# The sixth depthwise tile of a Conformer convolution: from TensorE to VectorE, ScalarE and POOL together

## The chip, the cores and the metric

One core of a Trainium2 chip runs the whole program in one launch. The metric is device time in microseconds (us) from start to end of one execution. A kernel is run several times, and medians are compared.

## The reference, cut to what matters

The program is a two-layer decoder trunk on 512 tokens of width 1024, in f32: each layer has two SwiGLU feed-forward blocks around a mixer, and a gated input embedding behind them. The mixer of layer 0 is a Conformer convolution, and the change lies inside it:

```python
def conformer_conv(h, w_pw1, b_pw1, w_dw, b_dw, ln_g, ln_b, w_pw2, b_pw2):
    u = h @ w_pw1 + b_pw1                     # 1024 -> 2048 channels
    a, g = jnp.split(u, 2, axis=-1)
    u = a * jax.nn.sigmoid(g)                 # the gate
    u = lax.conv_general_dilated(             # one causal filter of 31 taps per channel
        u, w_dw[:, None, :], window_strides=(1,), padding=[(CONV_KERNEL - 1, 0)],
        dimension_numbers=('NWC', 'WIO', 'NWC'), feature_group_count=D_MODEL) + b_dw
    mu = jnp.mean(u, axis=-1, keepdims=True)  # LayerNorm over the 1024 channels
    var = jnp.mean(jnp.square(u - mu), axis=-1, keepdims=True)
    u = (u - mu) * lax.rsqrt(var + LN_EPS) * ln_g + ln_b
    return jax.nn.silu(u) @ w_pw2 + b_pw2
```

The norm needs all 1024 channels of a token, so the second projection can't begin before the last channel's filter is done.

## The kernel before

Channels lie on the 128 partitions and tokens on the free axis: eight channel tiles c = 0 to 7 of 128 x 512. Every matrix product is made of three matmuls of rounded halves (`mm3`, lines 355 to 357). Weights come in units of 128 x 1024 in the order of use (`raw`, L243 on the queue of SP), and each is split in two: the high half by ScalarE (`wh`, L291), the low half by VectorE or, for the second projection of this stage, by POOL (`wl`, L293). Five split buffers go round, so a split waits until TensorE is done with the unit five before.

`conv` runs over the tiles. For each it makes the first projection (two banks of PSUM, 48 matmuls), then the gate (`glu`): VectorE scales (L732, L714), ScalarE applies the sigmoid (L715), VectorE multiplies. From there the tile's filter goes one of three ways, by the table `CONV_ON`:

- `pe`: the gated tile (L719) is written to DRAM (`ud`, L720) and read back rearranged by phase of the token (`uu`, L721). TensorE then makes the 31 taps with 36 matmuls against expanded taps (`tw`, four tiles of 576 KB per channel tile, L705; filter L817). ScalarE empties the bank (L822), and the result goes through DRAM again (`yd` L823, `y` L824).
- `dve`: the gated tile is written to SBUF with 30 zeros ahead (`u`, three buffers, L725, zeros L724). VectorE adds tap by tap in two PSUM banks (L744, L746), and joins them (L749, L750).
- `pool`: ScalarE scales the shifted tile by a tap (L759), POOL adds it to `y` (L760).

Behind each filter stands `tally`: the tile is added to a running sum (`total`, L774). After the first four tiles `centre` takes an estimate of the mean from the sum with a matmul (L785); from then on each tile also gets that mean taken off (L797), is squared on ScalarE (L803), and the square is added up (L804, the first four times on POOL).

The generators of `dve` and `pool` are pumped a few steps at a time between the projections (`PUMP`), the rest in a loop at the end of `conv`. While the last filters run, TensorE makes 16 small tiles of the input embedding (`z_tiles`; `fill`): each is 6 matmuls on `zp` into a bank of its own, emptied by ScalarE (L649) and sent to DRAM (L650). The end of the stage is: the sum's matmul (L903), the sums per token (L444, once for the total and once for the squares, six matmuls of `fill` between), the root on POOL (L437), and then per tile two steps of VectorE, the SiLU, the split (L925 to L929) and the second projection, whose matmuls are those on `tw` at L355 to L357.

What is written in this order is put through a list scheduler when the program is built. It fixes one order per engine and per queue, and on the chip each engine and queue works through its own order; an instruction that waits holds all behind it on its engine. `high_priority(FIN_PRI)` and `issue_after` are hints to that scheduler.

Of the kernel before, what the change touches and what calls it, by code (L numbers as in the profile page):

```python
# [14 lines left out]
AF = mybir.ActivationFunctionType  # L15
OP = mybir.AluOpType
# [5 lines left out]
TAPS = 31  # L22
X_W1, WARM = 4, 18
OUTS = 2
CONV_FIN = 0
PE_LATE = (3, 4, 5)
FIN_PRI = 100
CALM = ("ple_w_gate", "conv_w_pw2")
FIN_AT = (1, 3)
LATE, OUT_POOL, OUT_AFTER = 3, (1, 4), 2  # L30
PH, LAGS = 4, 9
CONV_ON = ("pool", "dve", "dve", "pe", "pe", "pe", "pe", "pe")
TAPS_AT = {max(0, c - 2): (c,) for c in range(8) if CONV_ON[c] == 'pe'}
TWB, PUMP = 8, {"dve": 5, "pool": 3, "pe": 0}
CENTRED = 2
FILL = (6, 0, 4, 3)
EARLY, SQP, PUMP2, ZIN = 4, 4, (12, 0), 6
CG, SP = 128 // PH, S // PH
# [18 lines left out]
def plan():  # L57
# [79 lines left out]
    for i in range(L):  # L137
        ffn(1, i)
        if i == 0:
            conv(0)  # L140
        else:
            nsa()
        ffn(2, i)
        full("ple_w_gate", i, KD, range(KD))
# [40 lines left out]
def phases(t):  # L185

    return t.rearrange("p (s r) -> p r s", r=PH)


def drain(gen):  # L190
    for _ in gen:
        pass


class Kern:
# [505 lines left out]
    def taps(self, c):  # L701

        T = [self.ptile("tw", TWB, 128 * LAGS) for _ in range(PH)]
        for q in range(PH):
            self.nc.sync.dma_start(T[q], self.a["tw"][CONV_ON[:c].count("pe"), q])  # L705
        return T

    def glu(self, c, pa, pg, ta=None):
# [4 lines left out]
        with self.tc.high_priority(FIN_PRI):  # L713
            nc.vector.tensor_tensor(pg, pg, self.R, op=OP.mult)  # L714
            nc.scalar.activation(pg, pg, AF.Sigmoid, bias=self.col("conv_b_pw1", KD + c))  # L715
            if CONV_ON[c] == "pe":
                u = self.ptile("uu", 2, PH * (SP + LAGS - 1)).rearrange("p (q s) -> p q s", q=PH)
# [35 lines left out]
    def dw_pool(self, c, u, y):  # L753
# [7 lines left out]
            yield  # L761
        self.tally(c, y)

    def tally(self, c, y):

        nc, b = self.nc, self.col("conv_b_dw", c)
        if not self.done:
            self.total = self.ptile("sum", 4)
            nc.vector.tensor_scalar(self.total, y, b, None, op0=OP.add)
        else:  # L770
            old = self.total
            if len(self.done) == EARLY:
                self.total = self.ptile("sum", 4)
            nc.vector.scalar_tensor_tensor(self.total, y, b, old, op0=OP.add, op1=OP.add)  # L774
        self.done.append((c, y))
        if self.mid is not None:
            self.square(c, y)
# [49 lines left out]
    def conv(self, nxt):  # L827

        nc = self.nc
# [3 lines left out]
        self.ud, self.yd = (self.dpool.tile([D, S], F32, name=n) for n in ("ud", "yd"))  # L833
        fin = self.rfin(self.acc)
        self.T, self.late, self.done, self.mid, self.squares, self.sqp = {}, [], [], None, None, SQP
        work = {"dve": self.dw_dve, "pool": self.dw_pool, "pe": self.dw_pe}
        queues = {on: [] for on in work}

        def pump(which, n):
            q = queues[which]  # L840
            while n > 0 and q:
                if next(q[0], q) is q:
                    q.pop(0)
                else:
                    n -= 1

        def filt(c, pa, pg, ta=None):
            u = self.glu(c, pa, pg, ta)
            Y.append(self.ptile("y", KD))
            queues[CONV_ON[c]].append(work[CONV_ON[c]](c, u, Y[c]))  # L850

        for c in range(KD):
# [13 lines left out]
            for p, o in ((pa, c), (pg, c + KD)):  # L866
# [5 lines left out]
                if p is pa:  # L872
                    ta = self.scaled(pa)
                if p is pg and c - 2 in PE_LATE:
                    drain(queues["pe"].pop(0))
                for on in queues:
                    pump(on, PUMP[on])
            filt(c, pa, pg, ta)
            if CONV_ON[c - 1] == "pe" and c - 1 not in PE_LATE:
                drain(queues["pe"].pop(0))  # L880

        def late(n):
            for _ in range(n):
                self.tally(*self.late.pop(0))
# [4 lines left out]
        fill = itertools.chain(*[self.z_tiles(i, ZP[i]) for i in range(L)])  # L889
        for _ in range(FILL[3]):  # L890
            next(fill)
# [1 line left out]
            drain(queues["pe"].pop(0))  # L893
        pump("dve", PUMP2[1])
        while any(queues.values()):
            for on, n in (("dve", 7), ("pool", 3)):
                pump(on, n)
        late(len(self.late))
        for _ in range(FILL[0]):
            next(fill)  # L900
        off, pt = self.bank(), self.bank()
        with self.tc.high_priority(FIN_PRI):
# [3 lines left out]
            u = self.tiny.tile([128, 4], F32, name="u", tag="u")  # L906
# [7 lines left out]
        nc.vector.tensor_tensor(off, off, self.mid, op=OP.subtract)  # L914
        for _ in range(FILL[1] + FILL[2]):
            next(fill)
# [4 lines left out]
        for c in range(KD):  # L921
            pair = self.ptile("tw", TWB, 128 * LAGS, F32R)
            h, l = pair[:, :512], pair[:, 512:1024]
            with self.tc.issue_after(ui if c < CENTRED else vi):
                nc.vector.tensor_tensor(Y[c], Y[c], off, op=OP.subtract)  # L925
# [546 lines left out]
def pack(inputs):  # L1472
# [17 lines left out]
    dw = taps[lag + PH].reshape(PH, LAGS, PH, KD, PH, CG).transpose(3, 4, 5, 0, 1, 2)  # L1490
    tw = np.zeros((CONV_ON.count("pe"), PH, CG, PH, LAGS, CG, PH), np.float32)
    for n, c in enumerate(c for c in range(KD) if CONV_ON[c] == "pe"):
# [33 lines left out]
```

## Time and profile before

| what | value |
|---|---|
| median of 3 runs | 2022.3 us (2020.97 to 2022.66) |
| the profiled execution's own time | 2022.25 us |
| its span in the trace | 2020.4 us |
| mean granted TensorE clock | 0.995 |
| busy: TensorE / VectorE / ScalarE / POOL | 99% / 77% / 54% / 16% |
| the convolution's stage | about 360 to 562 us of the span |

All times of trace rows count from the span's start. In rows of a timeline the columns are start, length, engine, line, operation, output<-inputs, shapes and count; merged rows give the length of the whole run of instructions. A bracket at the end tells how long the engine had been idle and what released it. PE is TensorE, DVE VectorE, ACT ScalarE, SPq the queue of DMAs that SP issues. In rows of the chain of work each row is a piece of the path that ended last. In rows of busy time by stretch the columns are the stretch, then its length, then busy time and number of instructions of PE, PEld, DVE, ACT and POOL, the granted clock, the DMA engines' share and GB/s.

### The profile page before, as it was taken

To read this page: it belongs to the slowest core of one execution; us is meant where nothing else is said; L and a number is where in the kernel's file an instruction comes from. 1 tells how busy PE (TensorE), PEld (TensorE's weight loads), DVE (VectorE), ACT (ScalarE), POOL (GpSimd) and SP (SyncE) were. 2 spreads that over 40 slices of the span, in tenths; PEclk is the share of its full clock that TensorE was granted. 3 is DMA by queue.
4 is the path that set the end of the run, shared out by engine and by line. 5 is a ranking of instruction groups with operands and counts; after the bars stand their busy time and mean duration, and the time that the engine had idled before them with its cause. 6 is when DMAs were issued, how large, how long until landed. Compare 5 with 4: busy or idle time off the path is not lost.

```text
span 2020.4 us, 32792 instructions
## 1 busy us (share of the span) xinstructions
PE 1993.4 (99%) x12534; PEld 1789.1 (89%) x12534; DVE 1559.0 (77%) x2751; ACT 1100.5 (54%) x1972; POOL 330.7 (16%) x365
## 2 busy tenths in 40 slices
PE   8999999999999999999999999999999999999998
PEld 7989899888789898988999989887888789898987
DVE  8869777795687796877968868647989796886875
ACT  7535445663565363545644535437888674463543
POOL 0000000352300000012000000557666200000022
PEclk9999999999999999999999999999999999999999
DMA  4332323466425244243232322463323023232241
GB/s 167 107 99 100 126 75 103 180 203 210 136 98 172 89 142 127 97 136 115 84 120 90 117 92 95 152 191 105 93 87 100 29 95 124 95 115 94 94 141 58
DMA packets 79484, 235.16 MB, mean 116 GB/s; under 512 B 8848, under 2 KB 16160, under 8 KB 79328
## 3 DMA queue, kind: packets, MB, share of 16 engines
q1 hardware_dynamic: 78368, 230.69, 34.8%
q8 instruction: 98, 1.61, 0.3%
q0 software_dynamic: 816, 2.33, 0.3%
q14 instruction: 58, 0.48, 0.1%
q10 hardware_dynamic: 144, 0.07, 0.0%
HBM read 214.66 MB, written 16.29 MB: 114 GB/s over the span
## 4 chain that ended last, share of the span: by engine, by line
PE 88%; DVE 7%; ACT 2%; DMA 1%; issue 1%; SPq 0%; DVEq 0%; POOL 0%; ACTq 0%
PE b L355 27%; PE b L356 27%; PE b L357 27%; PE b L817 2%; PE b L1176 1%; PE b L1238 1%; DMA raw<-in_w 1%; PE b L1257 1%; PE b L1115 1%; PE b L1258 1%; DVE t L1241 1%; DVE s L414 1%; DVE wl L293 1%; DVE t L481 0%; DVE acc L431 0%
## 5 line engine op out<-in xcount | busy, mean ns | idle before, releaser
L355 PE MATMUL b<-s,wh 128*128 128x256 f32 (+1 forms) x1408 | 447.9, 319 | 5.0 <-ACT wh L291 4.3
L356 PE MATMUL b<-s,wh 128*128 128x256 f32 (+1 forms) x1408 | 447.0, 318 | 1.3 <-DVE s L414 0.9
L357 PE MATMUL b<-s,wl 128*128 128x256 f32 (+1 forms) x1408 | 445.3, 318 | 0.5 <-DVE wl L293 0.4
L291 ACT ACTIVATE wh<-raw 128x1024 fp32r<-128x1024 f32 (+1 forms) x251 | 263.6, 1053 | 259.1 <-PE b L356 173.6
L355 PE MATMUL b<-px,wh 128*128 128x256 f32 (+1 forms) x1112 | 321.8, 290 | 0.8 <-ACT G L502 0.8
L356 PE MATMUL b<-px,wh 128*128 128x256 f32 (+1 forms) x1112 | 321.3, 289 | 0.8 <-DVE px L490 0.8
L357 PE MATMUL b<-px,wl 128*128 128x256 f32 (+1 forms) x1112 | 321.2, 289 | 0.0
L293 DVE TENSOR_TENSOR wl<-raw,wh 128x1024 fp32r<-128x1024 f32 (+1 forms) x205 | 251.3, 1227 | 69.6 <-ACT wh L291 68.9
L355 PEld LDWEIGHTS b<-s,wh 128*128 128x128 f32 x1408 | 267.7, 190 | 24.0 <-ACT wh L291 5.2
L356 PEld LDWEIGHTS b<-s,wh 128*128 128x128 f32 x1408 | 267.7, 190 | 19.9 <-DVE s L414 2.5
L357 PEld LDWEIGHTS b<-s,wl 128*128 128x128 f32 x1408 | 266.9, 190 | 18.3 <-DVE wl L293 1.1
L357 PE MATMUL b<-hid,wl 128*128 128x512 f32 x704 | 275.0, 393 | 0.0
L356 PE MATMUL b<-hid,wh 128*128 128x512 f32 x704 | 274.8, 392 | 0.0
L355 PE MATMUL b<-hid,wh 128*128 128x512 f32 x704 | 269.3, 390 | 0.0
L293 POOL TENSOR_TENSOR wl<-raw,wh 128x1024 fp32r<-128x1024 f32 (+1 forms) x53 | 128.4, 2427 | 709.4 <-ACT wh L291 709.2
L502 ACT ACTIVATE G<-b 128x256 f32<-128x256 f32 x400 | 144.6, 377 | 134.7 <-PE b L357 118.2
L355 PEld LDWEIGHTS b<-px,wh 128*128 128x128 f32 x1112 | 209.7, 189 | 6.4 <-ACT G L502 1.4
L356 PEld LDWEIGHTS b<-px,wh 128*128 128x128 f32 x1112 | 209.5, 188 | 5.9 <-DVE px L490 1.0
L357 PEld LDWEIGHTS b<-px,wl 128*128 128x128 f32 x1112 | 209.2, 188 | 3.8
L356 PEld LDWEIGHTS b<-hid,wh 128*128 128x128 f32 x704 | 132.2, 188 | 29.2
L355 PEld LDWEIGHTS b<-hid,wh 128*128 128x128 f32 x704 | 132.2, 188 | 28.5
L357 PEld LDWEIGHTS b<-hid,wl 128*128 128x128 f32 x704 | 132.1, 188 | 27.4
(246 smaller groups left out, 3644.7 us busy)
## 6 DMA issues: line engine op xcount, KB each, us to landing
raw<-in_w SPq DMA_DIRECT2D x255, 512.0 KB, 3.3
rawx<-in_w SPq DMA_DIRECT2D x80, 512.0 KB, 3.2
tw<-in_tw SPq DMA_DIRECT2D x20, 576.0 KB, 6.8
skew<-table SPq DMA_DIRECT2D x16, 320.0 KB, 5.9
z<-t SPq DMA_DIRECT2D x16, 256.0 KB, 2.3
hid<-z SPq DMA_DIRECT2D x16, 256.0 KB, 4.2
tt<-skew SPq DMA_DIRECT2D x16, 256.0 KB, 2.8
wr<-in_w SPq DMA_DIRECT2D x8, 512.0 KB, 4.2
```

The costliest lines, as they stand in the source:

```text
L291: nc.scalar.activation(h[:, c], t[:, c], AF.Copy)
L293: eng.tensor_tensor(l[:, c], t[:, c], h[:, c].bitcast(F32), op=OP.subtract)
L355: mm(out, sh, mh, start=start, stop=False, **how)
L356: mm(out, sh, ml, start=False, stop=False, **how)
L357: self.lastmm = mm(out, sl, mh, start=False, stop=stop, **how).ins
L414: b = nc.vector.scalar_tensor_tensor(view(l), x, g, view(h.bitcast(F32)), op0=OP.mult, op1=OP.subtract)
L502: copy = lambda o, x: nc.scalar.activation(o, x, AF.Copy)
L817: nc.tensor.matmul(p[:, q * SP:q * SP + SP], T[q][:, d * 128:d * 128 + 128], u[:, q, o:o + SP], start=d == 0, stop=d == LAGS - 1)
L1115: nc.tensor.matmul(P[mh][:, :124], w, B[kk // 4][:, kk % 4, :], start=kk == 0, stop=kk == 15)
L1176: nc.tensor.matmul(p[:, :32 - lo + nk], Q, KT[:, i, "sw".index(b), lo:32 + nk], start=i == 0, stop=i == 1)
L1238: nc.tensor.transpose(p[:, a * 128:a * 128 + 128], J[a, b][:, kt * 128:kt * 128 + 128], self.ident)
L1241: nc.vector.tensor_tensor(l, p, h.bitcast(F32), op=OP.subtract)
```

## The change

Tile 5 (the sixth) leaves the way `pe` for a fourth way, `mix`. Its gated tile is written to SBUF like a `dve` tile's. VectorE makes taps 0 to 15 in two PSUM banks; ScalarE scales for taps 16 to 30, and POOL adds 14 of these to `y` (the first is written there); then ScalarE brings the second bank to SBUF, POOL adds it, and VectorE adds the first bank to `y`.

```diff
-PE_LATE = (3, 4, 5)
+PE_LATE = (3, 4)
-CONV_ON = ("pool", "dve", "dve", "pe", "pe", "pe", "pe", "pe")
+CONV_ON = ("pool", "dve", "dve", "pe", "pe", "mix", "pe", "pe")
-TWB, PUMP = 8, {"dve": 5, "pool": 3, "pe": 0}
+TWB, PUMP = 8, {"dve": 5, "pool": 3, "pe": 0, "mix": 2}
+MIXED = 16
...
+    def dw_mix(self, c, u, y):
+        nc = self.nc
+        acc, n = [self.bank(), self.bank()], MIXED
+        for j in range(n):
+            a, w = acc[j % 2], self.dwc[:, c, j:j + 1]
+            if j < 2:
+                nc.vector.tensor_scalar(a, u[:, j:j + 512], w, None, op0=OP.mult)
+            else:
+                nc.vector.scalar_tensor_tensor(a, u[:, j:j + 512], w, a, op0=OP.mult, op1=OP.add)
+            if n + j < TAPS:
+                t = self.tmp() if j else y
+                nc.scalar.activation(self.rs(t), phases(u[:, n + j:n + j + 512]), AF.Copy,
+                                     scale=self.dwc[:, c, n + j:n + j + 1])
+                if j:
+                    nc.gpsimd.tensor_tensor(y, y, t, op=OP.add)
+            yield
+        t = self.tmp()
+        nc.scalar.activation(self.rs(t), phases(acc[1]), AF.Copy)
+        nc.gpsimd.tensor_tensor(y, y, t, op=OP.add)
+        nc.vector.tensor_tensor(self.rs(y), phases(acc[0]), self.rs(y), op=OP.add)
+        self.tally(c, y)
...
-        work = {"dve": self.dw_dve, "pool": self.dw_pool, "pe": self.dw_pe}
+        work = {"dve": self.dw_dve, "pool": self.dw_pool, "pe": self.dw_pe, "mix": self.dw_mix}
...
-            for on, n in (("dve", 7), ("pool", 3)):
+            for on, n in (("dve", 7), ("pool", 3), ("mix", 4)):
```

In the changed kernel lines 37 to 763 stand one lower than in the kernel before, and those behind 787 24 lower: L760 is now L761, L822 is L846, L903 is L927. The new way has L772 and L774 (taps on VectorE), L777 (scaling), L780 (POOL's add), L783 to L785 (the join).

The scheduler's order is moved at three places. The first is VectorE around the gate of tile 6 (its product is `t478_4431` before and `t474_4421` now). Before, taps of tile 2 (`u404`) stand around it:

```order
L774 SCALAR_TENSOR_TENSOR sum449_4265<-y422_4110,small_74,sum449_4265 128x512
L746 SCALAR_TENSOR_TENSOR b450_4267<-u404_3999,dwc_3711,b450_4267 128x512
L746 SCALAR_TENSOR_TENSOR b451_4268<-u404_3999,dwc_3711,b451_4268 128x512
L719 SCALAR_TENSOR_TENSOR t478_4431<-t478_4431,small_74,b476_4400 128x512
L746 SCALAR_TENSOR_TENSOR b450_4267<-u404_3999,dwc_3711,b450_4267 128x512
```

Now, with taps of tile 5 (`u457`) among them:

```order
L774 SCALAR_TENSOR_TENSOR b476_4432<-u457_4361,dwc_3711,b476_4432 128x512
L798 SCALAR_TENSOR_TENSOR sum445_4257<-y418_4102,small_74,sum445_4257 128x512
L774 SCALAR_TENSOR_TENSOR b477_4433<-u457_4361,dwc_3711,b477_4433 128x512
L747 SCALAR_TENSOR_TENSOR b446_4259<-u404_3999,dwc_3711,b446_4259 128x512
L720 SCALAR_TENSOR_TENSOR t474_4421<-t474_4421,small_74,b472_4390 128x512
```

From the join of tile 1 (L750) up to this gate VectorE has 10 taps of tile 5 that it had not, and 5 fewer of tile 2, which come later.

The second place is ScalarE behind the emptying of tile 7's filter bank. Before, the squares of tiles 5, 6 and 7 and the emptying of the `fill` banks follow:

```order
L822 ACTIVATE t514_4802<-b513_4765 128x512
L803 ACTIVATE t515_4808<-y462_4374 128x512
L803 ACTIVATE t516_4813<-y484_4525 128x512
L291 ACTIVATE wh520_4832<-raw87_4569 128x1024
L803 ACTIVATE t517_4818<-y493_4648 128x512
L649 ACTIVATE t519_4828<-b518_4821 128x512
```

Now the last seven scalings of tile 5 and its second bank stand there, the squares and the banks behind them:

```order
L846 ACTIVATE t517_4783<-b516_4746 128x512
L777 ACTIVATE t518_4788<-u457_4361,dwc_3711 128x512
L777 ACTIVATE t519_4792<-u457_4361,dwc_3711 128x512
L777 ACTIVATE t520_4796<-u457_4361,dwc_3711 128x512
L777 ACTIVATE t521_4800<-u457_4361,dwc_3711 128x512
L777 ACTIVATE t522_4804<-u457_4361,dwc_3711 128x512
L777 ACTIVATE t523_4808<-u457_4361,dwc_3711 128x512
L292 ACTIVATE wh531_4846<-raw87_4583 128x1024
L777 ACTIVATE t524_4812<-u457_4361,dwc_3711 128x512
L783 ACTIVATE t525_4816<-b477_4433 128x512
L292 ACTIVATE wh540_4892<-raw88_4715 128x1024
L827 ACTIVATE t526_4822<-y458_4364 128x512
```

So seven of the fifteen scalings can't begin before TensorE has ended the filter of tile 7. The third place is POOL at the same time. Before:

```order
L804 TENSOR_TENSOR sum499_4704<-sum499_4704,t505_4726 128x512
L293 TENSOR_TENSOR wl520_4833<-raw87_4569,wh520_4832 128x1024
L293 TENSOR_TENSOR wl529_4879<-raw88_4734,wh529_4878 128x1024
L437 TENSOR_TENSOR r_4909<-v_4905,power_78 128x4
L293 TENSOR_TENSOR wl540_4946<-raw89_4836,wh540_4945 128x1024
```

Now:

```order
L780 TENSOR_TENSOR y458_4364<-y458_4364,t521_4800 128x512
L294 TENSOR_TENSOR wl531_4847<-raw87_4583,wh531_4846 128x1024
L780 TENSOR_TENSOR y458_4364<-y458_4364,t522_4804 128x512
L294 TENSOR_TENSOR wl540_4893<-raw88_4715,wh540_4892 128x1024
L780 TENSOR_TENSOR y458_4364<-y458_4364,t523_4808 128x512
L780 TENSOR_TENSOR y458_4364<-y458_4364,t524_4812 128x512
L784 TENSOR_TENSOR y458_4364<-y458_4364,t525_4816 128x512
L438 TENSOR_TENSOR r_4923<-v_4919,power_78 128x4
```

Eight adds of tile 5 are left at that point (the first three, on `t518` to `t520`, stand just ahead of these rows), and two weight splits stand among them. On TensorE only the four rows of tile 5's filter are gone from between the first projection of tile 7 and the filter of tile 6; the 36 matmuls of `fill` between the filter of tile 7 and L903 stay where they were. On SP's queue the four `tw` loads and the four trips through DRAM of tile 5 are gone.

## The prediction

> **What bounds the kernel now.** I read the page's head first, then the table of busy time over the convolution, then what TensorE waits for there, then the chain of work.
>
> ```profile
> span 2020.4 us, 32792 instructions
> PE 1993.4 (99%) x12534; PEld 1789.1 (89%) x12534; DVE 1559.0 (77%) x2751; ACT 1100.5 (54%) x1972; POOL 330.7 (16%) x365
> sum 220.00, PE 219.01 PEld 185.47 DVE 158.10 ACT 127.62 POOL 75.43; mean PE 9.95 PEld 8.43 DVE 7.19 ACT 5.80 POOL 3.43
> 450.00:460.00 10.00, 10.00 (x64) 8.98 (x63) 10.00 (x15) 3.62 (x6) 0.51 (x2) 1.00 0.72 236
> PE b L355 <- ACT tw L928: 1.0, 1, 1.0
> ```
>
> The third row is 360 to 580 us: TensorE idles 1.0 us in 220, one wait at the start of the second projection. So the stage is bound by TensorE's work, and work taken from it is worth its length, provided nothing else becomes late. VectorE is the first candidate: in 450 to 460 (fourth row) it is busy throughout.
>
> ```profile
> 464.96 16.08 PE b L817 x144
> 481.04 0.86 PE b L785 x2
> 481.90 0.79 PE b L444 x8
> 487.01 8.04 PE b L817 x72
> 503.49 0.86 PE b L903 x2
> 504.34 0.79 PE b L444 x8
> 506.63 0.79 PE b L444 x8
> 517.36 1.20 PE b L355 x4
> ```
>
> These are pieces of the chain. The first row is tiles 5 and 6 back to back, the fourth tile 7. From the end of tile 7's filter (487.01 + 8.04 = 495.05) to L903 lie 8.44 us, filled by 36 matmuls of `fill`. That is all the cover that the last tally has.
>
> **The change, term by term.** *Removed.* Half of the first row, **-8.04 us** on the path. The four 576 KB loads and the trips through DRAM of tile 5 go from SP's queue; none was on the chain, so by themselves they bring nothing. L822 of tile 5 goes too.
>
> *Tile 6 moves up.* Its filter now stands at 464.96, where tile 5's stood. Is its input there? It comes from the gate on VectorE and two transfers.
>
> ```profile
> 437.90 1.06 DVE L750 TENSOR_TENSOR y<-b,t 128x512 f32<-128x512 f32 x1
> 442.17 4.69 DVE L746 SCALAR_TENSOR_TENSOR b<-u,dwc,b 128x512 f32<-128x512 f32 x7
> 459.01 0.73 DVE L719 SCALAR_TENSOR_TENSOR t<-t,small,b 128x512 f32<-128x512 f32 x1
> 472.41 0.75 DVE L719 SCALAR_TENSOR_TENSOR t<-t,small,b 128x512 f32<-128x512 f32 x1 [0.73 <-ACT b L715]
> 457.13 0.33 SPq L243 DMA_DIRECT2D raw<-in_w  x1
> 457.56 0.86 SPq L705 DMA_DIRECT2D tw<-in_tw  x2
> 459.77 0.33 SPq L720 DMA_DIRECT2D ud<-t  x1
> 465.34 0.37 SPq L721 DMA_DIRECT2D uu<-ud  x1
> 473.19 0.33 SPq L720 DMA_DIRECT2D ud<-t  x1
> 475.53 0.57 SPq L721 DMA_DIRECT2D uu<-ud  x1
> DMA to landing us min/median/max: 2.6/3.0/7.3
> ```
>
> The last row is that of `uu`. Between L750 and this gate the order has 10 taps more and 5 fewer; a tap takes 4.69 / 7 = 0.67, so 3.35, and the gate of tile 5 writes `u` instead of `t`, 0.4 more (1.12 against 0.74, below). There is no slack on VectorE to take that in, so tile 6's gate ends near 459.74 + 3.7 = 463.4. Before, from issuing `ud` to issuing `uu` took 5.57 for tile 6, behind three weight and tap loads, and 2.34 for tile 7, with free engines. Now two loads are ahead instead of three, and `ud` comes 3.7 later, so they are mostly through by then: I take 2.4, nearest tile 7's row. Landing at 463.4 + 2.4 + 3.0 = 468.8 gives a wait of 3.8; a little of the gate's delay is doubtful, and I take **+3.5** (ends: 0 if the transfers were as early as the filter, 7.1 with 5.57). Nothing else can run in it: TensorE's order has only this filter, then L785, then `fill`. Tile 7's gate is later by about as much (476), its transfers end at 476 + 2.4 + 3.0 = 481.4, and its filter starts at 464.96 + 3.5 + 8.04 + 0.86 + 0.79 + 4.3 of `fill` (481.90 + 0.79 to 487.01) = 482.5: just in time, no cost.
>
> *The clock.* A wait has a second price.
>
> ```profile
> 45.76 0.39 PE L355 MATMUL b<-s,wh 128*128 128x256 f32 x1 [3.10 <-ACT wh L291]
> 47.00:48.00 1.00, 1.00 (x5) 1.00 (x6) 1.00 (x3) 1.00 (x4) 0.00 (x0) 0.50 0.63 254
> 49.00:50.00 1.00, 1.00 (x8) 1.00 (x8) 1.00 (x3) 0.07 (x1) 0.00 (x0) 0.74 0.80 238
> 1582.40 0.69 PE L1238 MATMUL b<-ident,e 128*128 128x128 f32 x2 [2.41 <-POOL e L1218]
> 1588.00:1589.00 1.00, 1.00 (x4) 0.76 (x3) 0.97 (x3) 0.30 (x1) 1.00 (x4) 0.53 0.00 0
> ```
>
> After 3.10 us idle the granted clock (third figure from the end) was 0.50 and was back to 1.00 in the course of 49 to 50, 3.9 us after the restart by the 0.74; after 2.41 us idle it stayed low to 1589, 6.6 us. Half speed for 3.9 us loses 1.95. I charge **+1.9** for tile 6's wait (ends 0 and 3.3).
>
> The Trainium skill, TensorE: Matmul & The Clock Gate, section "What's actually happening", says that the array gets half of the pulses after an idle window of some 3.4 us and all again after about as long a busy one, in windows that run freely. By that rule a wait of 3.5 may or may not fill a window, and the sum would be without the 1.9 where it doesn't; the 2.41 row shows a drop after less, so the measurement speaks for charging it.
>
> *The tail of tile 5.* Everything that tile 5 adds to VectorE beside the two gates lies behind them and before L785, in time that was idle (the 9.41 us that VectorE waited for the centre, first row below). But seven scalings are queued on ScalarE behind the emptying of tile 7's bank, and eight adds and two splits on POOL behind these.
>
> ```profile
> 482.57 1.42 DVE L797 SCALAR_TENSOR_TENSOR y<-y,small,sum 128x512 f32<-128x512 f32 x2 [9.41 <-ACT sum L787]
> 414.34 6.80 ACT L759 ACTIVATE t<-u,dwc 128x512 f32<-128x512 f32 x6
> 495.15 0.60 ACT L822 ACTIVATE t<-b 128x512 f32<-128x512 f32 x1 [2.85 <-PE b L817]
> 504.88 1.08 ACT L291 ACTIVATE wh<-raw 128x1024 fp32r<-128x1024 f32 x1
> L760 POOL TENSOR_TENSOR y<-y,t x30: 1292/1300/2201, 383.7 to 448.8; 128x512 f32<-128x512 f32 x30
> L760 POOL TENSOR_TENSOR y<-y,t 128x512 f32<-128x512 f32 x30 | 44.6, 1488 | 33.2 <-ACT t L759 31.3
> L293 POOL TENSOR_TENSOR wl<-raw,wh 128x1024 fp32r<-128x1024 f32 x6 | 14.4, 2392 | 34.2 <-ACT wh L291 34.2
> L750 DVE TENSOR_TENSOR y<-b,t x2: 1064/1084/1103, 437.9 to 486.6; 128x512 f32<-128x512 f32 x2
> L725 DVE SCALAR_TENSOR_TENSOR u<-t,small,b 128x512 f32<-128x512 f32 x3 | 3.4, 1123 | 0.1
> L804 DVE TENSOR_TENSOR sum<-sum,t 128x512 f32<-128x512 f32 x3 | 2.1, 692 | 3.2 <-ACT t L803 3.1
> L774 DVE SCALAR_TENSOR_TENSOR sum<-y,small,sum x7: 737/752/1767, 452.1 to 500.8; 128x512 f32<-128x512 f32 x7
> ```
>
> Let E be the end of tile 7's filter. ScalarE empties its bank by E + 0.6, the first scaling ends at E + 1.8, six are through at E + 7.4 (6.80 / 6 = 1.13 each), the high half of a split at E + 8.4, the seventh scaling at E + 9.6, the bank copy at E + 10.7, the second high half at E + 11.8. POOL's four adds end at E + 1.8 + 4 x 1.30 = E + 7.0; it then waits until E + 8.4 for ScalarE, splits 2.4 to E + 10.8, adds to E + 12.1, splits 2.4 to E + 14.5, adds three times to E + 18.4. VectorE joins (1.08) to E + 19.5. Then come, one after another, the tally of tile 5 and its square's input (0.75 each), the same for tile 6, an add of squares (0.7) and the tally of tile 7: 4 x 0.75 + 0.7 + 0.75 = 4.5, and L903 starts at E + 24.0. It started at E + 8.44, so **+15.6** (lower end: the adds without the splits between, 8 x 1.30 from E + 1.8, 4.8 - 1.4 - 0.1 less, about +11; upper end: adds at the mean of 1.49, +1.5 more, +17). POOL's mean is the value under VectorE's load; in the tail VectorE waits for POOL, so I take the median.
>
> By the Trainium skill, GPSIMD Engine Reference, section "1. Specifications", POOL shares its SBUF interfaces with VectorE, with contention where that has two SBUF inputs; nothing of VectorE runs beside the tail's adds, so the sum by that rule is the same one with 1.30.
>
> *Behind L903.* TensorE has been idle for some 15 us, so the half clock is all but sure here. L903, L444, six matmuls and L444 of the squares took 506.63 - 503.49 = 3.14; with 3.9 us at half speed this becomes about 4.95: **+1.8** (ends 0.9, the emptying of a bank that now waits behind tile 7's square on ScalarE, and 3.0). From there to 517.36 VectorE and ScalarE set the pace (the 1.0 us wait), so slower `fill` matmuls are hidden.
>
> Sum: -8.04 + 3.5 + 1.9 + 15.6 + 1.8 = **+14.8 us**, on 2022.25 of the profiled execution (span 2020.4); the median of the runs, 2022.3, is the same within 0.05. Forecast **2037 us**, slower by 0.7%. A measurement of this kernel can tell about 0.2%, 4 us, from no change.
>
> **Rivals.**
>
> *The transfers are hidden and the clock forgives.* Tile 6's input arrives in time, nothing drops there: -8.04 + 15.6 + 0.9 = +8.5, 2031. For it speaks that fewer loads share the queue; against it that the gate alone is 3.7 late where the chain had 465.34 + 3.0 = 468.3 even before, which lies behind 464.96. Chance 0.12.
>
> *The removal pays.* The tail is hidden and 8.04 us are won: 2014. It decides at a tail of 8.44 + 8.04 = 16.5 us from E: below this the kernel is faster, and each microsecond of wait ahead takes one off. Even with both splits behind all adds, the eight adds, the lead of 1.8 and VectorE's 5.6 make 17.8. It needs scalings that run ahead of tile 7's filter, and ScalarE's order forbids that. Chance 0.04.
>
> *Break-even.* Tail near 18 and no wait of tile 6: -8.04 + 9.6 = +1.5, 2024. It needs the splits to cost nothing. Chance 0.05.
>
> *The shared port.* VectorE and POOL slow each other: POOL's adds took up to 2.2, and a tally 1.77 against 0.75. If this also hits the gate of tile 6 (four to five instructions at 1.0 more) and the adds run at 1.6: +14.8 + 2.4 + 4 = +21, 2043. For it: adds of tile 5 now run beside VectorE from 450 on. Against: most of VectorE's work then is taps, which took 0.67 each beside POOL at 442. Chance 0.09.
>
> **How the numbers follow.** The forecast holds 0.70, with its own range 2031 to 2041 from the ends above (no clock drop at tile 6 and a short wait; or a wait of 7). The first rival lies at 2031 and the port at 2043, and the range 2029 to 2042 leaves out the removal that pays, break-even and half of the port: under 0.2. Slower by over 0.2%: 0.70 + 0.12 + 0.09 and a little of break-even, 0.92; same 0.04; faster 0.04.
>
> **What would show it.** In the changed kernel's trace: L841 in three stretches of 8 us and the one of tile 6 starting near 468, with a wait for `uu` ahead; the granted clock at 0.50 behind it; L927 starting 24 us behind the end of the last L841, with a wait of some 15 us for VectorE, and VectorE's L785 waiting as long for POOL; the two L294 on POOL between the adds. The prediction is wrong if L927 follows its `fill` matmuls without a wait, or if TensorE's order at run time lets other work into the gap.

## Result, and the profile after

The changed kernel takes 2041.7 us (median of 4 runs, 2038.8 to 2043.5) against 2021.6 beside it: ratio 1.0095, 95% interval 1.0083 to 1.0107. That is 20 us slower, where 14.8 was forecast; the time lies 0.3 us inside the upper end of the range, 2029 to 2042. The profile below is of the slowest of the four executions (2043.5 us).

The page's head of the changed kernel:

```profile
span 2041.7 us, 32691 instructions
PE 1992.1 (98%) x12462; PEld 1786.4 (87%) x12462; DVE 1570.8 (77%) x2768; ACT 1117.5 (55%) x1987; POOL 350.3 (17%) x380
```

What its TensorE waited for between 360 and 600 us (total, times, longest):

```profile
PE b L927 <- DVE sum L798: 14.9, 1, 14.9
PE b L841 <- DMA uu<-ud: 7.1, 1, 7.1
```

Pieces of its chain of waits (start, length, what):

```profile
462.96 0.66 DVE t L720
463.63 5.67 DMA ud<-t
469.32 2.69 DMA uu<-ud
472.15 9.99 PE b L841 x72
488.09 8.05 PE b L841 x72
519.45 2.05 PE b L927 x2
521.50 1.50 PE b L445 x8
525.76 1.50 PE b L445 x8
```

TensorE is busy 1.3 us less in all and the span is 21.3 us longer: the time is waiting and slow clock, not work. Two waits are new. Tile 6's filter starts at 472.15 and not in tile 5's old place at 464.96; it then takes 9.99 in place of 8.04. L927 starts 23.3 us behind the end of tile 7's filter (488.09 + 8.05 = 496.14), where 8.44 had been.

The tail of tile 5, from the timelines of ScalarE, POOL and VectorE:

```profile
496.23 0.60 ACT L846 ACTIVATE t<-b 128x512 f32<-128x512 f32 x1 [2.78 <-PE b L841]
496.72 6.78 ACT L777 ACTIVATE t<-u,dwc 128x512 f32<-128x512 f32 x6
504.52 2.36 POOL L294 TENSOR_TENSOR wl<-raw,wh 128x1024 fp32r<-128x1024 f32 x1 [1.11 <-ACT wh L292]
506.85 1.25 POOL L780 TENSOR_TENSOR y<-y,t 128x512 f32<-128x512 f32 x1
508.06 2.33 POOL L294 TENSOR_TENSOR wl<-raw,wh 128x1024 fp32r<-128x1024 f32 x1
513.03 1.26 POOL L784 TENSOR_TENSOR y<-y,t 128x512 f32<-128x512 f32 x1
514.33 0.69 DVE L785 TENSOR_TENSOR y<-b,y 128x512 f32<-128x512 f32 x1 [23.05 <-POOL y L784]
```

It is the order that was foreseen: emptying, six scalings, the splits between the adds, and VectorE waiting 23.05 us for POOL.

The stage in stretches of four us (busy time of TensorE, its weight loads, VectorE, ScalarE and POOL, then granted clock, share of the DMA engines, GB/s), behind the restart at 519.45:

```profile
520.00:524.00 4.00, 4.00 (x13) 2.85 (x12) 1.86 (x3) 3.34 (x7) 0.00 (x0) 0.50 0.35 130
524.00:528.00 4.00, 4.00 (x15) 3.52 (x14) 0.70 (x3) 1.29 (x4) 0.00 (x0) 0.50 0.89 329
528.00:532.00 4.00, 4.00 (x14) 3.09 (x14) 4.00 (x9) 2.36 (x4) 1.02 (x1) 0.71 0.12 46
```

TensorE is busy in every microsecond from 520 on and still gets half the clock until about 530.3 (0.71 x 4 = 2.84, so 2.3 of the last four us at half), 10.9 us after it restarted.

The ledger of the stage, from the end of the projections to the start of the second one (517.36 before, 537.53 after, +20.2): filter removed -8.0, wait for `uu` +7.1, slow filter of tile 6 +1.95, tail +14.9, from L927 to the second projection +4.2. Sum 20.1. The remaining microsecond of the span lies scattered behind the stage.

### The profile page after: what moved, and what is told of

The parts are those of the page before. It is cut to its first block, busy times and chain, and to the rows that moved or that the text cites. A ratio compares the mean times of both kernels' runs of the same rounds, so it can differ in the third digit from the quotient of the medians.

```text
span 2041.7 us, 32691 instructions
## 1 busy us (share of the span) xinstructions
PE 1992.1 (98%) x12462; PEld 1786.4 (87%) x12462; DVE 1570.8 (77%) x2768; ACT 1117.5 (55%) x1987; POOL 350.3 (17%) x380
## 4 chain that ended last, share of the span: by engine, by line
PE 64%; DVE 11%; ACT 2%; issue 2%; DMA 1%; POOL 1%; SPq 0%; DVEq 0%; ACTq 0%; POOLq 0%
PE b L356 20%; PE b L357 20%; PE b L358 20%; DVE t L1265 1%; DVE b L747 1%; PE b L841 1%; DVE wl L294 1%; DVE e L1218 1%; PE b L1200 1%; PE b L1139 1%; ACT e L1220 0%; DVE s L415 0%; PE b L1262 0%; ACT t L1264 0%; DVE ect L1259 0%
```

## Experiments

The first three columns of the table come from all runs of a kernel; each ratio is to the kernel before in the same call, whose median was 2022.0 to 2022.5 for the experiments. The other columns come from one profile each, and a single execution can lie some us from its median (experiment 6's profile took 2045.5). "uu" is the wait of tile 6's filter and the filter's length by the timeline (8.20 with the whole clock, where the chain has 8.04, so that the changed kernel's 1.95 counts as 1.8 here); "tail" is the time from the end of tile 7's filter to L927 (8.27 before, by the rows of the timeline); "after" is the time from L927 to the second projection's first matmul.

```
kernel                          median   ratio (95%)               uu             tail    after
before                          2021.6   1                         0 + 8.2         8.3    14.0
changed                         2041.7   1.0095 (1.0083, 1.0107)   7.1 + 10.0     23.3    18.1
1 steps earlier                 2041.5   1.0095 (1.0080, 1.0110)   3.6 + 9.9      22.2    19.7
2 steps later, gate first       2046.6   1.0120 (1.0105, 1.0135)   2.1 + 9.9      32.4    19.7
3 splits on VectorE             2038.2   1.0078 (1.0063, 1.0093)   7.0 + 9.9      19.7    19.3
4 TensorE kept busy             2037.2   1.0076 (1.0059, 1.0093)   3.8 + 9.9      23.7    14.6
5 all steps ahead               2029.6   1.0037 (1.0024, 1.0049)   5.6 + 11.2     11.2    17.0
6 uu first                      2041.3   1.0090 (1.0074, 1.0105)   6.9 + 10.7     23.3    18.4
7 removal alone                 2021.1   0.9995 (0.9986, 1.0004)   3.6 + 11.0      8.3    14.0
8 all ahead, fill and uu first  2026.2   1.0022 (1.0013, 1.0031)   2.7 + 9.7      11.2    17.0
9 taps loaded later             2042.9   1.0102 (1.0088, 1.0115)   5.0 + 11.0     23.3    18.6
10 joining ahead too            2023.1   1.0006 (0.9997, 1.0015)   6.4 + 10.0      8.3    14.0
11 10 with fill and uu first    2019.7   0.9988 (0.9979, 0.9996)   2.5 + 9.7       8.3    14.0
12 10 with fill, two taps later 2021.3   0.9994 (0.9985, 1.0003)   3.9 + 10.9      8.3    14.0
```

The theory at the outset: the tail comes from where tile 5's last steps stand in the queues, and the other loss from tile 6's input. Rivals: the steps are too much work wherever they stand, or VectorE and POOL slow each other.

### 1. The steps written earlier

```diff
         self.centre()
+        pump("mix", MIXED + 1)
         pump("dve", PUMP2[0])
```

> The tail of tile 5 comes from where its last steps are written (seven scalings stand on ScalarE behind the emptying of tile 7's bank), not from how long the scalings and adds take. With all of them written ahead of it, L927 should start about 8.4 us behind the end of tile 7's filter, as in the kernel before (8.44), with no wait of its own (14.9 now); the clock behind it then stays whole, since TensorE is no longer idle ahead of it. Left over are the removed filter (-8.04), the wait of tile 6's filter (+7.1) and its slow clock (+1.95), so about 2021.6 + 1.0 = 2023 us (2021 to 2026). Rival: the scalings, the adds or the crowding of VectorE by POOL are simply too long for the stage; then more than half of the 14.9 us stays in front of L927 and the time is above 2031.

The order was as meant: all scalings stood ahead of the emptying of tile 7's bank. It brought nothing. From the timelines of ScalarE and TensorE:

```profile
475.29 0.66 ACT L716 ACTIVATE b<-b,small 128x512 f32<-128x512 f32 x1 [8.54 <-DVE b L715]
483.25 8.00 ACT L777 ACTIVATE t<-u,dwc 128x512 f32<-128x512 f32 x7
507.37 0.61 ACT L846 ACTIVATE t<-b 128x512 f32<-128x512 f32 x1
499.89 0.79 PE L356 MATMUL b<-zp,wh 128*128 128x512 f32 x1 [6.20 <-DVE y L785]
514.49 2.04 PE L928 MATMUL b<-sum,meanr 128*128 128x512 f32 x2 [4.46 <-DVE sum L798]
```

The seven scalings still stood behind tile 7's gate, for which ScalarE idled 8.54 us, and behind the squares, so they began at 483.25 and not 496.7. What they gained, two others lost: tile 5's two PSUM banks were held until its joining, so `fill` found no bank (6.20), and tile 7's own emptying stood on ScalarE behind the squares of tiles 5 and 2 and three emptyings of `fill` banks until 507.37. The tail is 22.2, by another road. My expectation was wrong, and by this run alone the rival "too much work" would stand.

### 2. The same, with none of tile 5's taps ahead of tile 6's gate

```diff
-TWB, PUMP = 8, {"dve": 5, "pool": 3, "pe": 0, "mix": 2}
+TWB, PUMP = 8, {"dve": 5, "pool": 3, "pe": 0, "mix": 0}
```

on top of the edit above.

> As with all steps of tile 5 written ahead of tile 7's emptying, and besides none of its VectorE taps ahead of tile 6's gate (ten stand there in the changed kernel). The gate on VectorE should end some 3.3 us sooner, tile 6's filter wait about 3.8 us rather than 7.1, so the time is 2 to 4 us under that of the version with the steps early alone: about 2019 us (2017 to 2023). Rival: the wait hangs on the two transfers' own length, not on the gate; then both versions agree within 1 us. A second way to lose: 16 taps on VectorE behind the gate end late, tile 5's join holds L927 back, and the time is above 2025.

What TensorE waited for between 430 and 600 us:

```profile
PE b L356 <- DVE y L785: 7.8, 1, 7.8
PE b L356 <- ACT t L783: 7.3, 1, 7.3
PE b L841 <- DMA uu<-ud: 2.1, 1, 2.1
```

The gate came 3.9 us sooner (`ud` issued at 459.74, 463.63 in the changed kernel) and the wait for `uu` fell to 2.1. TensorE waited for both of tile 5's banks, 7.3 us for the one that L783 frees and 7.8 for the other, where experiment 1 had one wait of 6.2, and the tail grew to 32.4. The second way to lose that was named is what happened.

### 3. Two of POOL's splits made on VectorE

```diff
+ON_DVE = [j for j, u in enumerate(UNITS) if u[0][0][0] == "conv_w_pw2"][1:3]
...
+        calm = calm and j not in ON_DVE
         eng = nc.gpsimd if calm or nsa and j % 4 in L_POOL else nc.vector
```

> Two of the second weight's splits (2.36 and 2.33 us) stand between tile 5's last adds on POOL. Made on VectorE, which waits 23 us for POOL there, they leave the adds to follow ScalarE's scalings: the last add ends some 4.5 us earlier, L927 with it, and the time is about 2037 us (2036 to 2038.5). Rival: the chain is bound by ScalarE's scalings and the splits only fill POOL's idle time; then the time stays within 1 us of the changed kernel (2041.7).

Median 2038.2, the wait for VectorE's sum 11.3 in place of 14.9 (-3.6; two splits of 2.35 are 4.7). The splits are in the path of the tail. Why not all of the 4.7 came back shows in POOL's adds (shortest, median and longest in ns) and in VectorE's first split:

```profile
L782 POOL TENSOR_TENSOR y<-y,t x7: 1289/1297/2282, 497.3 to 506.4; 128x512 f32<-128x512 f32 x7
503.77 1.39 DVE L296 TENSOR_TENSOR wl<-raw,wh 128x1024 fp32r<-128x1024 f32 x1 [13.20 <-ACT wh L294]
```

Against the expectation the adds did not follow ScalarE's scalings: POOL ran them back to back, and the last one began at 506.37, 1.5 us after its scaling had ended. Five took 1.29 to 1.30, but the two that ran beside VectorE's splits (503.77 to 505.16 and 506.31 to 507.54) took 2.13 and 2.28. VectorE and POOL slow each other here, and that took back 1.8 us.

### 4. TensorE kept busy during the tail

```diff
         off, pt = self.bank(), self.bank()
+        self.keep_warm(off, 60)    # 60 matmuls of 128x512 on meanr, overwritten behind
```

> 60 matmuls of 128x512 whose result nobody reads stand on TensorE ahead of L927, while it waits 14.9 us there. If the half clock behind L927 is what the squares and the stage's end lose there (3.2 + 1.6 us), the clock stays at 1.00 behind it and the time is about 2041.7 - 4.8 = 2037 us (2036 to 2039); the wait of tile 6's filter and its slow clock stay. Rival: VectorE and ScalarE set the pace behind L927 whatever the clock, as the prediction said: then at most 1.8 us come back (2040 or more).

TensorE's timeline:

```profile
502.77 13.94 PE L833 MATMUL b<-meanr 128*128 128x512 f32 x60 [1.52 <-ACT t L783]
516.55 1.02 PE L932 MATMUL b<-sum,meanr 128*128 128x512 f32 x2
531.11 1.20 PE L356 MATMUL b<-tw,wh 128*128 128x512 f32 x4 [0.99 <-ACT tw L957]
```

The tail is as long as in the changed kernel (23.7), L932 takes 1.02 and not 2.05, and from there to the second projection lie 14.6 us in place of 18.1, with 14.0 in the kernel before. So the half clock behind the tail cost 3.5 us, and it is TensorE's speed that cost them, since nothing else was changed. The median, 2037.2, is what was expected.

### 5. All of tile 5's steps ahead of tile 7's gate

```diff
-TWB, PUMP = 8, {"dve": 5, "pool": 3, "pe": 0, "mix": 2}
+TWB, PUMP = 8, {"dve": 5, "pool": 3, "pe": 0, "mix": 4}
```

> One number: four steps of tile 5 instead of two are written per half of a later tile's product, so that all its taps, scalings and adds stand ahead of the emptyings of tiles 6 and 7, in the stretch 459 to 480 where ScalarE idled 8 us and POOL 12 us in the version with the steps early. There the last seven scalings began only at 483.25, behind tile 7's gate and the squares of the finished tiles, which is why moving them earlier by a few places brought nothing. If the queue position is what makes the tail, L927 now starts 8.4 us behind the end of tile 7's filter, without a wait, the clock behind it stays whole, and what is left is the removed filter (-8.04), tile 6's wait (+3.6 to +7.1, as measured in five profiles) and its slow clock (+1.95): 2019 to 2023 us, most likely 2021. Rival: the amount of work on ScalarE and POOL makes the tail wherever it stands (as the version with the steps early might suggest): L927 again more than 20 us behind, 2037 or more.

Between the two: the tail fell from 23.3 to 11.2, which the rival excluded, but not to 8.4. Timelines of VectorE, POOL and ScalarE:

```profile
496.18 0.59 ACT L783 ACTIVATE t<-b 128x512 f32<-128x512 f32 x1
498.09 2.41 POOL L294 TENSOR_TENSOR wl<-raw,wh 128x1024 fp32r<-128x1024 f32 x1
503.59 2.50 POOL L294 TENSOR_TENSOR wl<-raw,wh 128x1024 fp32r<-128x1024 f32 x1 [3.09 <-ACT wh L292]
498.90 2.14 DVE L798 SCALAR_TENSOR_TENSOR sum<-y,small,sum 128x512 f32<-128x512 f32 x1
503.80 2.83 DVE L798 SCALAR_TENSOR_TENSOR sum<-y,small,sum 128x512 f32<-128x512 f32 x1
462.93 0.74 DVE L720 SCALAR_TENSOR_TENSOR t<-t,small,b 128x512 f32<-128x512 f32 x1
```

Two things were left. The joining (L783) still stood behind the emptying of tile 7's bank. And the sums behind it met POOL's splits: L798 took 2.14 and 2.83 in place of 0.75. Each of the two ends 0.54 us behind POOL's split (500.50 and 506.09), as if it had been held until then. That fits the contention of the Trainium skill, GPSIMD Engine Reference, section "1. Specifications" (shared SBUF interfaces, where VectorE has two SBUF inputs): it shows at L798, which reads `y` and `sum` from SBUF, and not at L720, one of whose inputs lies in PSUM, and which took 0.74 beside POOL's adds.

### 6. uu ahead of the reading back on SP's queue

The edit, cut to its sense:

```diff
-        nc.sync.dma_start(y, self.yd[c * 128:c * 128 + 128, :])
+        # kept back until the next tile's uu is issued:
+        with self.tc.issue_after(self.uu):
+            self.nc.sync.dma_start(y, self.yd[c * 128:c * 128 + 128, :])
```

> Only the order on SP's queue: the load of tile 6's input (uu) is issued ahead of the reading back of tile 4's output (y from yd), which in the changed kernel stands in front of it and waits until yd has landed (8.6 us there, 8.0, 5.2 and 5.1 us in three other profiles of the same place). If that queue position makes tile 6's wait vary from 3.6 to 7.1 us, uu is issued about 2 us behind ud in every run, the wait is about 3.5 us (7.1 in the changed kernel's profile), and the median falls by 1 to 3 us, to 2039 to 2041. Rival: ud itself takes 5.7 us to land; then the wait stays at 7 in some runs and the median at 2041.7.

SP's queue:

```profile
460.55 0.39 SPq L847 DMA_DIRECT2D yd<-t  x1
464.15 0.33 SPq L721 DMA_DIRECT2D ud<-t  x1
469.77 0.37 SPq L722 DMA_DIRECT2D uu<-ud  x1
470.23 0.46 SPq L856 DMA_DIRECT2D y<-yd  x1
```

The reading back no longer stands in front, and `uu` still goes out 5.6 us behind `ud`. The position behind the reading back is not the cause; `ud` itself lands late.

### 7. The removal alone

```diff
     def dw_mix(self, c, u, y):
-        ... (taps, scalings, adds, joining)
+        yield
+        nc.vector.tensor_scalar(self.rs(y), phases(u[:, 0:512]), self.dwc[:, c, 0:1], None, op0=OP.mult)
         self.tally(c, y)
```

> Tile 5's filter is left out: one scaling on VectorE stands for its 31 taps, so the output leaves that part of the computation out. It tells what the removal alone is worth, with nothing new on VectorE, ScalarE and POOL. No tail and no loss of clock behind L927 (8.4 us behind the end of tile 7's filter); tile 6's filter is still 8 us sooner, and its input comes 3.3 us sooner at most: a wait of 2 to 5 us, its slow clock 0 to 1.95. So 2021.6 - 8.04 + 2 to 7 = 2016 to 2021, most likely 2018. Rival: without the taps the input is there in time, and the whole 8 us is won: 2014.

2021.1, just above what was expected, and 1.4 us under the kernel before (2022.45) in the same call, with an interval that includes no change. TensorE's timeline:

```profile
467.86 10.96 PE L825 MATMUL b<-uu,tw 128*128 128x128 f32 x72 [3.62 <-DMA uu<-ud]
```

With nothing put in its place, the removed filter of 8.04 us is worth some 1.4, which can't be told from nothing: in this profile tile 6's input is late by 3.62, and the slow clock behind that wait lengthens its filter by 2.8 (10.96 against 8.20). -8.04 + 3.62 + 2.76 = -1.7. A replacement can hardly win much more without help for tile 6. This is one profile, though, and over all profiles the wait lay between 2.1 and 7.1 us.

### 8. All steps ahead, uu first, and two fill tiles ahead of tile 6's filter

```diff
+            if c == KD - 1:
+                fill = itertools.chain(*[self.z_tiles(i, ZP[i]) for i in range(L)])
+                for _ in range(2):
+                    next(fill)
             if CONV_ON[c - 1] == "pe" and c - 1 not in PE_LATE:
                 drain(queues["pe"].pop(0))
```

with the edits of 5 and 6.

> All of tile 5's steps ahead and uu first on SP's queue, and two of the three fill tiles are written ahead of tile 6's filter instead of behind it (6 matmul groups, about 2.7 us), so that TensorE works while uu is on its way. Tile 6's wait should be about 1 us, too short to cost the clock, and nothing is left of the tail: 2021.6 - 8.04 + 1 to 3 = 2015 to 2018 us, most likely 2016.5, the first version under the kernel before by more than its noise. Rival: the fill holds banks that tile 6's filter or the gate of tile 7 needs, and what it covers comes back as another wait: 2019 to 2022.

2026.2: 3.4 us better than 5, still behind the kernel before, and 10 us from the expectation and beyond its rival's 2022; the expectation took the tail for gone before 5 had been seen. The tail is that of 5. The fill covers part of the wait, 2.7 is left, and the filter still takes 9.7.

### 9. Tile 7's taps loaded later

```diff
-TAPS_AT = {max(0, c - 2): (c,) for c in range(8) if CONV_ON[c] == 'pe'}
+TAPS_AT = {max(0, c - 2 * (c < 7)): (c,) for c in range(8) if CONV_ON[c] == 'pe'}
...
+            with self.tc.issue_after(self.uu) if c == 7 else nullcontext():
                 self.nc.sync.dma_start(T[q], self.a["tw"][CONV_ON[:c].count("pe"), q])
```

> The four loads of tile 7's filter (576 KB each) go out behind the load of tile 6's input instead of at 452 to 460, where they are in flight when tile 6's gate is written to DRAM (ud) and tile 4's output (yd). Putting uu ahead of the reading back on SP's queue left ud's way at 5.6 us, so the queue position is not it. If the big loads ahead of ud on the DMA engines are, ud lands about 2.0 to 2.5 us behind its issue (as tile 7's does, 2.0), tile 6's filter waits about 3.7 us in place of 7.1, and the time falls by 2 to 3.5 us from 2041.5, to about 2039. Rival: the writing to DRAM itself takes 5 to 6 us there (VectorE and POOL busy with SBUF beside it, or yd's own writing): then the wait stays near 7 and the time at 2041.5; and a second: tile 7's taps come too late and its filter waits, then the time is above 2042.

SP's queue and TensorE's timeline:

```profile
463.93 0.38 SPq L722 DMA_DIRECT2D ud<-t  x1
467.03 0.37 SPq L723 DMA_DIRECT2D uu<-ud  x1
469.90 10.98 PE L842 MATMUL b<-uu,tw 128*128 128x128 f32 x72 [5.04 <-DMA uu<-ud]
```

`ud` is through in 3.1 us, without tile 7's loads ahead of it, and the wait is 5.0 in place of 7.1. That gain is smaller than expected, the filter took 1.0 longer, and the time did not fall (2042.9; the intervals overlap). The second rival is not the reason: tile 7's filter started without a wait. The big loads are a part of the late landing at most.

Where `ud` spends its time shows in the movement of data (last two figures: mean share of the 16 DMA engines, GB/s). First the changed kernel, then the one with TensorE kept busy, in which the same transfer took 2.3 us:

```profile
464.00:465.00 1.00, 1.00 (x5) 0.56 (x3) 1.00 (x3) 1.00 (x2) 0.92 (x2) 1.00 1.11 356
466.00:467.00 1.00, 0.00 (x0) 0.00 (x0) 1.00 (x3) 0.56 (x2) 0.97 (x1) 1.00 0.07 27
467.00:468.00 1.00, 0.00 (x0) 0.00 (x0) 1.00 (x2) 0.66 (x1) 0.95 (x1) 1.00 0.06 23
```

```profile
464.00:465.00 1.00, 1.00 (x5) 0.56 (x3) 1.00 (x3) 1.00 (x2) 0.92 (x2) 1.00 1.08 350
466.00:467.00 1.00, 0.00 (x0) 0.00 (x0) 1.00 (x3) 1.00 (x2) 0.93 (x1) 1.00 0.69 102
```

In the changed kernel a share of 0.06 to 0.07, one engine of sixteen, works on from 465.5 to 469 while the others are done; in the other profile all were done at 465.6, and the next transfer was under way before 467. A transfer is there when its last part is: in all 14 profiles `uu` goes out 0.3 to 0.4 us behind the last packet of `ud`.

The packets in the changed kernel's trace show what that engine did. It took its shares in the order in which SP had issued the transfers: from 465.55 the last four packets of the weight load issued at 459.13 (4096 bytes each), from 466.18 eight of the `tw` load (4608), from 467.58 thirty-two of `yd` (512), and only from 468.33 to 468.98 its eight of `ud` (2048). In experiment 6 the last engine shows the same order. So 2.8 us of `ud`'s way went into what lay ahead of it on one engine: the transfers issued ahead of it did count, unlike the place of the reading back. Why that engine was so far behind is not settled. The way differs from profile to profile: 5.7, 2.3, 4.8, 5.1, 2.3, 3.6 and 5.6 us from issuing `ud` to issuing `uu` in the changed kernel and experiments 1 to 6 are one profile each, and experiments 7 to 12 gave 5.5, 3.6, 3.1, 3.6, 3.5 and 3.1.

### 10. The joining ahead of the squares too

```diff
-TWB, PUMP = 8, {"dve": 5, "pool": 3, "pe": 0, "mix": 2}
+TWB, PUMP = 8, {"dve": 5, "pool": 3, "pe": 0, "mix": 4}
...
         nc.vector.tensor_tensor(self.rs(y), phases(acc[0]), self.rs(y), op=OP.add)
+        yield
         self.tally(c, y)
...
+        pump("mix", 1)
         late(max(0, EARLY - len(self.done)))
```

> All of tile 5's steps ahead, and its joining too: it stands in front of the squares of the finished tiles, where VectorE idles 3.5 us, instead of behind the emptying of tile 7's bank. With the steps ahead but the joining not, L927 stood 11.4 us behind the end of tile 7's filter, because L783 (0.58) and L784 (1.30) came only at 496.2, and VectorE's sums behind them (2.14 and 2.83 instead of 0.75) ran beside POOL's weight splits. Now the sums of tile 5 are done before, L927 starts 8.4 us behind, without a wait, the clock behind it stays whole, and the way from L927 to the second weight's product is 14.0 us again, as before the change. What is left is the removed filter, tile 6's wait and its clock (-8.04 + 3.6 to 7.1 + 2 to 3.2): 2020 to 2024 us, most likely 2021.5. Rival: VectorE and POOL hinder each other wherever the steps stand; then it stays near 2029.6.

TensorE's timeline:

```profile
471.03 10.02 PE L842 MATMUL b<-uu,tw 128*128 128x128 f32 x72 [6.42 <-DMA uu<-ud]
486.86 8.20 PE L842 MATMUL b<-uu,tw 128*128 128x128 f32 x72
503.33 1.02 PE L929 MATMUL b<-sum,meanr 128*128 128x512 f32 x2
517.37 1.19 PE L356 MATMUL b<-tw,wh 128*128 128x512 f32 x4 [0.99 <-ACT tw L954]
```

The whole filter on three engines, all 31 taps, and the tail is that of the kernel before: 503.33 lies 8.27 behind the end of tile 7's filter, and the second projection starts at 517.37 where it started at 517.36. So the tail was a matter of order alone: the work is the same in both kernels. The time, 2023.1, is the same as before: the removed 8.0 are used up by 6.4 of waiting and 1.8 of slow clock at tile 6.

### 11 and 12. The same, with cover for tile 6's input

The eleventh is 10 with the edits of 6 and 8 (two fill tiles first, `uu` first). The twelfth is 10 with the fill first and two of tile 7's four tap loads behind `uu`.

> The version with the fill first and uu first (2026.2), with tile 5's joining ahead of the squares as well. It should lose the 2.9 us of late start and the 3.0 us of slow way behind L927 that were left: about 2020 us (2018 to 2022), under the kernel before by about its noise. Rival: tile 6's wait (2.7 there) and a new wait at tile 7's filter eat it: 2022 to 2024.

> As the version with the joining ahead and the fill first, but in place of uu first two of tile 7's four filter loads go out behind the load of tile 6's input. If those loads hold ud up, tile 6's input lands while the fill runs, its filter does not wait and keeps the clock; tile 7's filter may then wait 1 to 2 us for its own input. About 2018 us (2016 to 2020.5), faster than before by more than the noise. Rival: ud's way is not shortened by it; then it equals the version with uu first.

```profile
469.75 9.74 PE L842 MATMUL b<-uu,tw 128*128 128x128 f32 x72 [2.52 <-DMA uu<-ud]
513.74 1.20 PE L356 MATMUL b<-tw,wh 128*128 128x512 f32 x4 [0.99 <-ACT tw L967]
```

The eleventh, whose rows these are, starts the second projection 3.6 us sooner than the kernel before, of which the profiled span keeps 1.6, and runs in 2019.7, as expected: 2.3 us less than the kernel before in the same call, ratio 0.9988 (0.9979 to 0.9996). It is the only version whose interval lies below 1, by 0.04%. That is one interval of twelve, and under the 0.2% that the prediction takes a measurement to tell, so a gain is likely and not shown. The twelfth, 2021.3, cannot be told from no change and misses what was expected of it: SP issued `ud` only at 464.64, behind the landing of `yd`, and in spite of the fill the wait was 3.9. The trace puts its end down to a tap on VectorE (L775, ended at 470.60), but `uu` had landed only some 0.2 us before that.

## Why the prediction came out as it did

- *The time.* 2041.7 is inside the range and 4.7 above the forecast. The forecast's own range ended at 2041; the rest up to 2042 was there for half of the shared port, which is not what happened. So that the time lies inside owes something to luck, since two terms below were too small by 6 us together.
- *Removed filter, -8.04.* Right on the path. Without the tail and what is behind L903 the prediction's terms leave -2.6; experiment 7 measured -1.4, with no change inside its interval.
- *Gate of tile 6 at 463.4.* It ended at 463.6. Right.
- *Wait for `uu`, +3.5.* Mis-sized: 7.1, the upper end. The step that failed is the choice of 2.4 for the way of `ud`, "nearest tile 7's row". It was 5.7 here, and 5.57 had been measured for the same tile at nearly the same time (459.77) in the kernel before. Fewer loads ahead did not make it tile 7's case. Over the changed kernel and experiments 1 to 6 it took 2.3 to 5.7, so the wait has no single value; the middle of its range was the better estimate, and its upper end belonged in the range, where it was.
- *Slow clock at tile 6, +1.9.* 9.99 - 8.04 = 1.95. Right that the clock drops; that the size fits is partly chance. In the experiments the filter took 1.5 to 3.0 longer than 8.20, and not by the length of the wait: 1.7 after a wait of 3.57 (experiment 1) and 2.8 after 3.62 (experiment 7). The row at 45.76 gives 3.8 us at half clock by its 0.74, not 3.9.
- *Tail, +15.6.* 23.3 - 8.4 = 14.9. Right, and by the road described: emptying, scalings, two splits among the adds, joining. VectorE's joining took 0.69, not 1.08. The lower end of about +11 does not follow from its own figures: 1.8 + 8 x 1.30 + 5.6 is E + 17.8, or +9.4, as the rival "Break-even" has it. Experiments 1 and 5 correct the reason given for it. The queue position behind L846 is one of three: tile 7's gate and the squares hold the scalings back as well, and the joining has a place of its own. Experiment 10 shows the rest: with another order nothing of the tail is left.
- *Behind L903, +1.8.* Mis-sized: 4.2 (3.14 with 1.95 lost would in any case be 5.09, not 4.95). The failed step is "slower `fill` matmuls are hidden". The clock stayed at half for 10.9 us after the restart, not for 3.9, so `fill` and the squares' sums on TensorE came to set the pace, and keeping TensorE busy (experiment 4) gave back 3.5.
- *Rivals.* "The removal pays" needed scalings that run ahead; experiment 10 has them and stands at 1.0006, because tile 6's wait takes the gain, as that rival's price said (each microsecond of wait takes one off), and its slow clock besides. The shared port showed itself in experiment 5 at 1.4 and 2.1 us on two sums of VectorE and in experiment 3 at 0.8 and 1.0 us on two adds of POOL; in the changed kernel nothing of VectorE ran beside POOL in the tail, and the gate of tile 6 (L720) took 0.73, as before.

The three terms that were off, +3.6, -0.7 and +2.4, add to +5.3; with the clock's 0.05 and the 1.1 us behind the stage this is the distance from +14.8 to the +21.3 of the profiled execution's span.

## What to carry to other kernels

Work taken off the bounding engine is worth its length only if the next piece can start that much sooner: price the next piece's input, and the slow clock behind its wait, before the replacement. For this filter spread over three engines the order of each queue counted more than the work: what must be early (the joining, the release of banks) has to be written ahead of everything that waits for something later. For a transfer's way take the row of the same transfer at the same time, or the whole range of its measured values, and not that of a quieter one.

## What the hardware did that I had not expected

- Half clock comes in steps. In every trace here a stretch at half clock, but for the one at the program's end, lasts 3.41 us or a whole multiple of it, up to 23.89. Behind a restart with the dense filter the whole clock was back after 3.0 to 6.2 us (3.4 in experiment 2, 6.2 in experiment 5), by where the restart fell in these steps.
- Behind a restart with L927 and the 128x1 matmuls of L445 it took longer: 10.9 us in the changed kernel, 11 to 12 in experiments 1, 2, 3, 6 and 9, 7.8 in experiment 8 and 7.3 in experiment 5, with TensorE busy throughout. The Trainium skill, TensorE: Matmul & The Clock Gate, section "What's actually happening", gives at least one busy window of some 3.4 us, in windows that run freely, for the return; behind L927 the measurement is two to three and a half times that. In all eight profiles the steps that held 1.4 us or more of L445's matmuls stayed at half, and the first later one, with at most 0.3 us of them, brought the clock back. Where the clock was whole (the kernel before, experiments 4, 7, 10, 11 and 12), the same matmuls did not bring it down. That these small matmuls are the cause is argued from this, not tested.
- The clock dropped after idle times as short as 2.13 us (experiment 2) and 2.52 (experiment 11), and the filter behind it lost 1.7 and 1.5 us. After 1.52 us, ahead of the 60 matmuls of experiment 4, it did not drop.
- A 256 KB transfer took from 2.3 to 5.7 us at the same place of nearly the same program; in the longest one of sixteen DMA engines was still at work for 3.4 us behind the others, with shares of earlier transfers ahead of its own.
